# Two pairs of gate/up groups, each by seven products of 512 columns, in place of four single groups by seven products of 256

## The chip, the cores and the metric

The kernel runs on one core of one Trainium2 chip. The metric is the device time of one execution in microseconds. In three runs the kernel before took 278.68, 278.72 and 279.11 us, with a median of 278.72 us. One execution was recorded by the hardware profiler: it took 278.33 us, of which the instructions span 276.6 us, at a mean granted TensorE clock of 0.995. All times of instructions below are of that execution, in us from the start of the span.

The engines are named as in the profile: PE (TensorE; PEld is its weight load), DVE (VectorE), ACT (ScalarE), POOL (GpSimd) and SP (the engine whose queue issues most loads).

## The reference

The program is one transformer block on 256 tokens of width 1024, all in float32:

```python
u = rms_norm(h, mix_norm_g[l])
proj = u @ w_in[l]                      # q, k, v, glu_a, glu_g
attn_out = moba_attention(heads(q), heads(k), heads(v), rel_bias)
conv_out = conformer_conv(glu_a, glu_g, ...)
h = h + concatenate([attn_out, conv_out]) @ w_out[l]
u = rms_norm(h, ffn_norm_g[l])
h = h + (silu(u @ w_gate[l]) * (u @ w_up[l])) @ w_down[l]
return rms_norm(h, final_norm_g)
```

The change lies in the feed-forward part, the last two lines but one: `u @ w_gate` and `u @ w_up` are products of 256 x 1024 by 1024 x 2816, and `w_down` is 2816 x 1024.

## The kernel before

**Precision.** Every float32 operand is cut into a high part, which a cast rounds to the multiply format (ACT, `act.copy`), and a low part, the rest (DVE, `vec.tensor_sub`). A product is three matmuls: high by high, high by low, low by high. Tiles `wh_*` are the high parts of weights; all low parts lie in nine slots of one tile, `wl`. `split(name)` makes both parts of one loaded block, `high(name, i)` only the high part of one half. A loaded block (`raw_*`) is two halves of 128 x 1024 elements, 512 KB each.

**Groups.** The 2816 columns of gate and up are 11 groups `g` of 256 columns. A plain group (`gate_up`) takes 48 matmuls of 512 moving columns, 256 of gate and 256 of up side by side, into two PSUM banks `pf`, one for each 128 tokens. `swiglu` takes Silu on ACT (`fs`) and the product on DVE (`ff`).

**Seven products.** Groups 4, 6, 8 and 10 (`SG`) are computed by a seven-multiplication scheme of Strassen's kind instead: the 256 tokens are two blocks, the depth of 1024 two blocks, the columns two blocks, and instead of eight block products there are seven, of sums of blocks. The sums of token blocks are made once (`sums_of_blocks`, tile `sf`). The sums of weight blocks, seven *forms* for each group, are made on DVE (`ft` tiles hold them) and cut into high and low parts as other weights are (`form`; tiles `wh_m*`). Each of the seven products is 12 matmuls of 256 columns. ACT copies finished products out of PSUM and DVE adds them (`cp` tiles). `first_forms`, `middle_forms` and `last_forms` stand at three places ahead of the products; the parts of a group are made one to two groups ahead.

**Way back to the down projection.** The gated product `ff` must be turned, tokens against columns. `send(g)` transposes blocks on DVE (`fv`), writes them to DRAM from POOL's queue (`fd`) and reads them back in four transfers (`fb`). `land(g)` makes their high part on ACT (`fh`) and low part on DVE (`fl`). `down(g, ...)` is 24 matmuls of 512 columns for a group, added up over all groups in four PSUM banks `pd`. Each product of `down` is three matmuls, by `fh` and `wh_d`, `fh` and `wl`, then `fl` and `wh_d`.

**Order.** The order on each engine is the order of the program text (`tc.keep_in_program_order`): an instruction whose input is late holds up all that stand behind it on its engine. The loop over groups writes, for each `g`: `swiglu(g)` and `send(g)`, the products of group `g+1`, the parts of group `g+2`, `land(g-1)` and `down(g-1)`. Loads are issued by SP in the order of the list `order` as buffers come free: `raw` has room for three blocks. PSUM has four banks beside those of `pd`, taken in turn (`spare`). `h_turn`, `h_rows` and `h_back` turn the residual stream through DRAM for the end (tiles `hb`, `ht`); two of its eight transposes on DVE are made in each of groups 1 to 4.

Of the kernel before, what the change touches and what calls it, by code (L numbers as in the profile page):

```python
# [15 lines left out]
P = 128  # L16
# [26 lines left out]
SG = (4, 6, 8, 10)  # L43
MIX = 48

# [19 lines left out]
def block_kernel(ctx, tc, xT, w_in, w_out, w_gu, w_down, pvec, gfin, relb, hot, out):  # L65
# [37 lines left out]
    for g in range(FG + 2):  # L103
        if g < FG:
            order += [(w_gu, 4096 * g, f"g{g}"), (w_gu, 4096 * g + 2048, f"u{g}")]
        if g > 1:
            order += [(w_down, 2048 * (g - 2), f"d{g - 2}")]
# [161 lines left out]
    def diagonal(rc, name):  # L269
        dg = const.tile([P, S], F32, name=f"dg_{name}", tag="dg")  # L270
# [10 lines left out]
    def sumsq(a, src, k, n):  # L281
        if k == 0:
            act.activation(a, src, AF.Square)
        else:
            sq = const.tile([P, S], F32, name=f"sq_{n}{k}", tag="sq", bufs=3)
            act.activation(sq, src, AF.Square)
            vec.tensor_add(a, a, sq)
# [113 lines left out]
    def bias_parts():  # L401
        pzs.append(const.tile([2 * NB, S], F32R, name="hot_r", tag="sq", bufs=3))
# [281 lines left out]
    def seven_products(g):  # L684
# [5 lines left out]
        kept = [w2.tile([P, 512], F32, name=f"cp{g}{i}", tag="fsq", bufs=2) for i in range(2)]  # L690
# [32 lines left out]

    def swiglu(g):
# [143 lines left out]
    def square_rows(t, i, lo, hi):  # L868
        sq = w2.tile([P, 512], F32, name=f"fsq{t}{i}", tag="fsq", bufs=2)
# [10 lines left out]
    def last_columns(t):  # L880
# [11 lines left out]
        sq = w2.tile([P, 512], F32, name=f"fsq{t}2", tag="fsq", bufs=2)  # L892
# [77 lines left out]
def _layout(x, mix_norm_g, w_in, rel_bias, conv_w, conv_b, conv_ln_g, conv_ln_b, w_out,  # L970
# [13 lines left out]
    gu = _in_turns(np.concatenate(pairs, axis=3)).reshape(P, FG, -1)  # L984
    for n in SG:
# [34 lines left out]
```

## Time and profile before

| what | value |
|---|---|
| median of 3 runs | 278.72 us |
| the profiled execution | 278.33 us |
| its span, first to last instruction | 276.6 us |
| PE / DVE / ACT / POOL busy, share of the span | 97% / 88% / 66% / 19% |
| one plain group on PE | 10.36 us |
| one group by seven products on PE | 9.38 us |
| one group's down projection on PE | 5.18 us |
| the feed-forward products begin / the last one by seven products ends | 109.44 / 253.25 us |

The profile's rows give a start, a length, the engine, the operation and the tiles it writes and reads (`out<-in`), how many instructions are merged, and in brackets how long the engine had been idle and what released it. Instructions on DVE and ACT overlap a little at their ends, so what one costs in a row of them is the step from start to start, not the length. The chain of waits is followed back from the last instruction; a chain that stays on one engine without a break means that this engine set the end.

### The profile page before, as it was taken

The page shows a single profiled execution, that of the slowest core. Times are in us where ns is not written, and L with a number is a line of the kernel's source. Part 1 is how long each engine was busy: PE and PEld are TensorE (multiplying, and loading weights), DVE is VectorE, ACT ScalarE, POOL GpSimd, SP SyncE. Part 2 cuts the span into 40 slices and gives each one's busy share as a digit, 9 for nine tenths or more (in the row PEclk, how much of TensorE's full clock was granted, in tenths as well). Part 3 has the DMA queues.
Part 4 walks back from the last instruction along what each step waited for, and adds up shares of the span by engine and source line. Part 5 has one row for each costly group of instructions (what it writes and reads, how often), then busy time and mean ns, then how long its engine had stood idle before and what let it go on. Part 6 is the DMA issues. An engine that isn't in the chain of part 4 may idle for free.

```text
span 276.6 us, 5114 instructions
## 1 busy us (share of the span) xinstructions
PE 268.0 (97%) x1845; PEld 243.1 (88%) x1845; DVE 243.2 (88%) x432; ACT 183.5 (66%) x317; POOL 52.0 (19%) x89
## 2 busy tenths in 40 slices
PE   8999999999999999999999999999999999999990
PEld 8999996996899998888888998899888998899880
DVE  3998999999977789979999699998969998988684
ACT  4894676996796678779655566657647684766331
POOL 2011000041001000331421403140430413140052
PEclk9999999999999999999999999999999999999998
DMA  7999899999938455894995468969894688961012
GB/s 219 346 378 346 302 242 277 359 251 221 294 120 261 144 196 162 290 368 135 317 382 182 154 213 283 331 169 283 254 393 142 217 292 309 354 236 28 0 47 105
DMA packets 22811, 66.38 MB, mean 240 GB/s; under 512 B 3258, under 2 KB 6274, under 8 KB 22786
## 3 DMA queue, kind: packets, MB, share of 16 engines
q1 hardware_dynamic: 18754, 55.08, 58.6%
q0 software_dynamic: 3600, 10.57, 14.6%
q10 hardware_dynamic: 432, 0.41, 0.4%
q8 instruction: 14, 0.23, 0.3%
q14 instruction: 11, 0.09, 0.1%
HBM read 58.10 MB, written 5.32 MB: 229 GB/s over the span
## 4 chain that ended last, share of the span: by engine, by line
PE 90%; DVE 4%; DMA 1%; issue 1%; ACT 1%; SPq 1%; POOL 0%; POOLq 0%; DVEq 0%; ACTq 0%
PE pf L77 23%; PE pd L77 19%; PE ps L77 15%; PE py L77 8%; PE pqk L77 8%; PE pv L77 4%; PE pa L77 4%; PE pg L77 3%; PE pc L77 3%; DMA raw_a<-in_w_in 1%; PE pt L80 1%; DVE acch L88 1%; PE po L77 1%; DVE hg L88 1%; DVE wl L88 1%
## 5 line engine op out<-in xcount | busy, mean ns | idle before, releaser
L77 PE MATMUL pf<-wl,us 128*128 128x512 f32 x112 | 42.4, 379 | 0.0
L77 PE MATMUL pf<-wh_u,us 128*128 128x512 f32 x112 | 34.7, 380 | 0.0
L77 PE MATMUL pf<-wh_g,us 128*128 128x512 f32 x112 | 34.5, 379 | 0.0
L77 PE MATMUL pd<-wh_d,fh 128*128 128x512 f32 x84 | 32.0, 381 | 0.0
L88 POOL DMA_DIRECT2D fb<-fd x40 | 23.2, 586 | 46.7 <-issue 25.1
L77 PE MATMUL pd<-wl,fh 128*128 128x512 f32 x84 | 31.8, 379 | 0.0
L77 PE MATMUL pd<-wh_d,fl 128*128 128x512 f32 x84 | 31.8, 379 | 0.0
L88 DVE TENSOR_TENSOR wl<-raw_d,wh_d 128x1024 fp32r<-128x1024 f32 x22 | 26.1, 1214 | 2.7 <-ACT wh_d L88 2.3
L88 ACT CAST wh_m<-ft 128x1024 fp32r<-128x1024 f32 x16 | 16.8, 1048 | 15.3 <-DVE ft L88 15.2
L77 PEld LDWEIGHTS pf<-wh_g,us 128*128 128x128 f32 x112 | 21.2, 189 | 3.0
L77 PEld LDWEIGHTS pf<-wh_u,us 128*128 128x128 f32 x112 | 21.2, 189 | 3.0
L77 PEld LDWEIGHTS pf<-wl,us 128*128 128x128 f32 x112 | 21.2, 189 | 3.0
L88 ACT CAST wh_d<-raw_d 128x1024 fp32r<-128x1024 f32 x22 | 22.6, 1048 | 0.9 <-DMA raw_d<-in_w_down 0.6
L77 PE MATMUL ps<-wh_m,sf 128*128 128x256 f32 x128 | 22.7, 275 | 0.0
L77 PE MATMUL pqk<-us,wh_qk 128*128 128x256 f32 x128 | 21.7, 276 | 0.0
L77 PEld LDWEIGHTS ps<-wh_m,sf 128*128 128x128 f32 x128 | 20.1, 192 | 0.0
L77 PEld LDWEIGHTS pqk<-us,wh_qk 128*128 128x128 f32 x128 | 19.5, 192 | 0.5 <-issue 0.4
L88 DVE SCALAR_TENSOR_TENSOR cacc<-upad,pv,cacc 128x256 f32<-128x256 f32 x48 | 19.8, 479 | 0.0
L88 DVE TENSOR_TENSOR wl<-ft,wh_m 128x1024 fp32r<-128x1024 f32 x16 | 19.0, 1212 | 0.0
L77 PE MATMUL ps<-wh_m,us 128*128 128x256 f32 x96 | 18.0, 275 | 0.0
L77 PE MATMUL py<-mh,wh_o 128*128 128x256 f32 x64 | 18.0, 281 | 0.0
L77 PEld LDWEIGHTS pd<-wh_d,fl 128*128 128x128 f32 x84 | 15.9, 189 | 2.2
(184 smaller groups left out, 736.2 us busy)
## 6 DMA issues: line engine op xcount, KB each, us to landing
raw_g<-in_w_gu SPq DMA_DIRECT2D x22, 512.0 KB, 5.0
raw_u<-in_w_gu SPq DMA_DIRECT2D x22, 512.0 KB, 5.1
raw_d<-in_w_down SPq DMA_DIRECT2D x22, 512.0 KB, 5.6
raw_qk<-in_w_in SPq DMA_DIRECT2D x8, 512.0 KB, 7.3
raw_o<-in_w_out SPq DMA_DIRECT2D x8, 512.0 KB, 6.4
raw_a<-in_w_in SPq DMA_DIRECT2D x12, 256.0 KB, 4.2
fd<-fv POOLq DMA_DIRECT2D x10, 256.0 KB, 4.8
fb<-fd POOLq DMA_DIRECT2D x40, 64.0 KB, 4.7
```

Source lines behind the costliest of these rows:

```text
L77: return tc.keep_in_program_order(nc.tensor.matmul(*args, **kw))
L80: return tc.keep_in_program_order(nc.tensor.transpose(o, i, ident))
L88: return lambda *a, **k: tc.keep_in_program_order(f(*a, **k))
```

## The change

Groups 4+5 and 8+9 (the program counts from zero) are now computed in pairs (`PAIRS`), groups 6 and 10 become plain, and `SG` is empty. So there are seven plain groups before and after, and four groups by seven products.

In a pair the column blocks are gate and up of both groups, 512 columns each. Each form is 512 deep by 512 wide, that is two halves of 128 x 1024 elements (`form(g, (i, n), ...)`), and each product is two half products of 6 matmuls of 512 columns (`half_product`). The pair has 14 halves of forms and 8 passes for sums, as two single groups had. Its products fill four PSUM banks (`x`, `y`, `z`, `w`); the copies, sums and gates work on 512 columns at a time.

The forms are split round a plain group's product: form 0 and the first sums stand behind the plain group's parts (`first_of_pair`), form 1 ahead of that group's `swiglu` (`forms_of_sums`), forms 2 and 3 and the other sums behind it (`middle_of_pair`), and forms 4, 5 and 6 inside the products, ahead of the first three (`late`). `down` of two groups follows a pair. `send` of a pair issues both writes ahead of the reads. The residual's transposes move: two in each of groups 1 and 2, four in group 6, with `h_rows` and `h_back` there too. Some small tiles change pools, and `hb`, `ht` and the unsummed blocks share one buffer.

```diff
@@ -40,8 +40,11 @@
 WARM = 9
 SHIFT = 16
 PLACE = 112
-SG = (4, 6, 8, 10)
+PAIRS = (4, 8)
+SG = ()
 MIX = 48
+TURNS = {1: (0, 1), 2: (2, 3), 6: (4, 5, 6, 7)}
+ROWS, BACK = 6, 6
 
 PROGRAM = """
...
@@ -100,11 +103,12 @@
     places.update({f"v{i}": (w_in, 16384 + 2048 * i) for i in range(2)})
     places.update({f"o{i}": (w_out, 2048 * i) for i in range(4)})
     order = [(*places[t[1]], t[1]) for t in steps if t[0] == "ld" and t[1] in places]
-    for g in range(FG + 2):
-        if g < FG:
-            order += [(w_gu, 4096 * g, f"g{g}"), (w_gu, 4096 * g + 2048, f"u{g}")]
-        if g > 1:
-            order += [(w_down, 2048 * (g - 2), f"d{g - 2}")]
+    units = [(g, g + 1) if g in PAIRS else (g,) for g in range(FG) if g - 1 not in PAIRS]
+    for unit in units:
+        names = ("ga", "gb", "gd", "gc") if len(unit) > 1 else ("g", "u")
+        order += [(w_gu, 4096 * unit[0] + 2048 * i, f"{n}{unit[0]}") for i, n in enumerate(names)]
+        order += [(w_down, 2048 * (g - 2), f"d{g - 2}") for g in unit if g > 1]
+    order += [(w_down, 2048 * g, f"d{g}") for g in range(FG - 2, FG)]
     order.reverse()
     raws, parts = {}, {}
     low = wts.tile([P, 9 * HW + 128], F32R, name="wl", bufs=1)
...
@@ -647,10 +655,39 @@
             form(g, 4 + i, raw)()
 
 
+    def first_of_pair(g):
+        a, b, d = (take(n + str(g)) for n in ("ga", "gb", "gd"))
+        for n in range(2):
+            form(g, (0, n), a[n])()
+        t = [[w2.tile([P, HW], F32, name=f"ft{g}{i}{n}", tag="ft", bufs=4) for n in range(2)] for i in range(2)]
+        for n in range(2):
+            vec.tensor_sub(t[0][n], b[n], a[n])
+        for n in range(2):
+            vec.tensor_sub(t[1][n], d[n], b[n])
+        raw4[g] = t, d
+
+    def forms_of_sums(g, i):
+        lows = [form(g, (1 + i, n), raw4[g][0][i][n]) for n in range(2)]
+        for low_part in lows:
+            low_part()
+
+    def middle_of_pair(g):
+        t, d = raw4[g]
+        c = take(f"gc{g}")
+        forms_of_sums(g, 1)
+        for n in range(2):
+            vec.tensor_sub(t[0][n], d[n], t[0][n])
+        for n in range(2):
+            form(g, (3, n), c[n])()
+        for n in range(2):
+            vec.tensor_sub(t[1][n], c[n], t[0][n])
+        raw4[g] = t[0], d, t[1]
+
     sums = []
...
@@ -721,6 +758,79 @@
             send(g)
             split(f"u{g + 1}")
 
+    def half_product(o, g, i, n, uh, ul, start):
+        wh, wl = forms[g, (i, n)]
+        for k in (2 * n, 2 * n + 1):
+            h, l = (in_turns(w[:, k % 2 * 512 : k % 2 * 512 + 512]) for w in (wh, wl))
+            mm(o, uh[:, k], h, start=start and k == 0, stop=False, skip_group_check=True)
+            mm(o, uh[:, k], l, start=False, stop=False, skip_group_check=True)
+            mm(o, ul[:, k], h, start=False, stop=k == 3, skip_group_check=True)
+
+    def pair_products(g):
+        sf = sums[1]
+        u = [[tuple(p[:, 4 * k : 4 * k + 4, t * P : (t + 1) * P] for p in (hh, hl)) for k in range(2)] for t in range(2)]
+        m = [(sf[:, i, 0], sf[:, i, 1]) for i in range(4)]
+        x, y, z, w = (bank(next(spare), f"ps{n}{g}") for n in "xyzw")
+        s1, s5, s7, su = (w2.tile([P, 512], F32, name=f"cp{g}{i}", tag="fsq", bufs=4) for i in range(4))
+        first, second, nxt = f"d{g - 2}", f"d{g - 1}", g + 2
+
+        def late(i, n):
+            form(g, (i, n), raw4[g][i - 4][n])()
+
+        def gate(t, a, b):
+            act.activation(a, a, AF.Silu, scale=rc2[:, t : t + 1])
+            for i in range(2):
+                ff[g + i, t] = a[:, i * S : (i + 1) * S]
+            return lambda: vec.tensor_mul(a, a, b)
+
+        late(4, 0)
+        half_product(x, g, 0, 0, *u[0][0], True)
+        late(4, 1)
+        half_product(x, g, 0, 1, *u[0][0], True)
+        act.copy(s1, x)
+        land(g - 2)
+        late(5, 0)
+        half_product(y, g, 1, 0, *m[0], True)
+        late(5, 1)
+        half_product(y, g, 1, 1, *m[0], True)
+        act.copy(s5, y)
+        late(6, 0)
+        half_product(z, g, 2, 0, *m[2], True)
+        late(6, 1)
+        half_product(z, g, 2, 1, *m[2], True)
+        act.copy(s7, z)
+        split(first, 0)
+        half_product(w, g, 3, 0, *u[0][1], True)
+        split(first, 1)
+        vec.tensor_add(s5, s5, s7)
+        half_product(w, g, 3, 1, *u[0][1], True)
+        vec.tensor_add(s1, w, s1)
+        split(second, 0)
+        half_product(x, g, 4, 0, *m[1], False)
+        high(second, 1)
+        half_product(x, g, 4, 1, *m[1], False)
+        act.copy(su, x)
+        split(second, 1)
+        high(f"g{nxt}", 0)
+        vec.tensor_add(s5, s5, su)
+        half_product(y, g, 5, 0, *m[3], False)
+        high(f"g{nxt}", 1)
+        split(f"g{nxt}", 0)
+        half_product(y, g, 5, 1, *m[3], False)
+        vec.tensor_add(s7, y, su)
+        one = gate(0, s1, s7)
+        one()
+        split(f"g{nxt}", 1)
+        half_product(z, g, 6, 0, *u[1][1], False)
+        land(g - 1)
+        high(f"u{nxt}", 0)
+        half_product(z, g, 6, 1, *u[1][1], False)
+        vec.tensor_add(su, z, su)
+        two = gate(1, su, s5)
+        two()
+        send(g, g + 1)
+        split(f"u{nxt}")
...
@@ -733,12 +843,17 @@
     fd = [dram.tile([4, 2, P, 2 * 32], F32, name=f"fd{n}") for n in range(3)]
     fb = {}
 
-    def send(g):
-        fv = w2.tile([P, 4, 2, 2 * 32], F32, name=f"fv{g}", tag="fv", bufs=2)
-        for t in range(2):
-            vec.transpose(fv[:, :, t], ff[g, t])
+    def send(*groups):
+        for g in groups:
+            fv = w2.tile([P, 4, 2, 2 * 32], F32, name=f"fv{g}", tag="fv", bufs=2)
+            for t in range(2):
+                vec.transpose(fv[:, :, t], ff[g, t])
+            pool.dma_start(fd[g % 3].rearrange("b t p c -> p (b t) c"), fv.rearrange("p b t c -> p (b t) c"))
+        for g in groups:
+            receive(g)
+
+    def receive(g):
         d = fd[g % 3]
-        pool.dma_start(d.rearrange("b t p c -> p (b t) c"), fv.rearrange("p b t c -> p (b t) c"))
         fb[g] = w2.tile([P, 2, 4, 2, 32], F32, name=f"fb{g}", tag="fb", bufs=3)
         for b in range(4):
             pool.dma_start(fb[g][32 * b : 32 * b + 32].rearrange("p t a i s -> p (t a) (i s)"),
...
@@ -804,44 +921,54 @@
 
 
 
-    for g in range(FG):
-        if g not in SG:
+    for unit, after, then in zip(units, units[1:] + [()], units[2:] + [(), ()]):
+        g = unit[-1]
+        ahead = len(then) > 1
+        shared = [n[0] for n in (after, then) if n]
+        shared = [n in SG or n in PAIRS for n in shared] + [False, False]
+        if not (g in SG or len(unit) > 1 or len(after) > 1):
             swiglu(g)
-            if g < FG - 1:
+            if after:
                 send(g)
-        if g + 1 in SG:
+        if len(after) > 1:
+            pair_products(g + 1)
+        elif shared[0]:
             last_forms(g + 1)
             seven_products(g + 1)
         else:
-            if g < FG - 1:
+            if after:
                 gate_up(g + 1)
-            if 0 < g < FG - 1:
+            if g > 0 and (after or g not in SG):
                 split(f"d{g - 1}")
-            if g + 2 in SG:
-                first_forms(g + 2)
-            elif g < FG - 2:
-                split(f"g{g + 2}")
+            if shared[1]:
+                first_forms(then[0])
+            elif then:
+                split(f"g{then[0]}")
             if g > 0:
                 land(g - 1)
-        if 0 < g < FG - 2:
-            for i in range(2):
-                for t in range(2):
-                    for n in range(2):
-                        down(g - 1, i, t, n * 512, n * 512 + 512)
-        if g + 2 in SG:
-            middle_forms(g + 2)
-        elif g < FG - 2 and g + 1 not in SG:
-            split(f"u{g + 2}")
+        for n in range(g - 1, g - 1 + len(after)):
+            if 0 <= n < FG - 3:
+                for i in range(2):
+                    for t in range(2):
+                        for c in range(2):
+                            down(n, i, t, c * 512, c * 512 + 512)
+        if ahead:
+            forms_of_sums(then[0], 0)
+            swiglu(g + 1)
+            send(g + 1)
+        if shared[1]:
+            middle_forms(then[0])
+        elif then and not shared[0]:
+            split(f"u{then[0]}")
         if g == 0:
             sums_u()
             sums_of_blocks()
-        if g == 8:
+        for m in TURNS.get(g, ()):
+            h_turn(m)
+        if g == ROWS:
+            h_rows()
+        if g == BACK:
             h_back()
-        if 1 <= g <= 4:
-            h_turn(2 * g - 2)
-            h_turn(2 * g - 1)
-        if g == 4:
-            h_rows()
     split(f"d{FG - 1}")
 
 
```

How the instructions stand now. First DVE, around the end of a pair's products. In front of the low parts `fl3`, which down(3) reads, there stood before (`u5` and `g6` are blocks of gate/up weights, `d3` of down weights, `ft6*` sums for the forms of group 6):

```order
L88 TENSOR_TENSOR wl_69<-raw_u5_0_2001,wh_u5_0_2109 128x1024
L88 TENSOR_TENSOR wl_69<-raw_u5_1_2002,wh_u5_1_2110 128x1024
L88 STREAM_TRANSPOSE hb_1495<-xs_70 128x8x32 x2
L88 TENSOR_TENSOR wl_69<-raw_d3_0_2050,wh_d3_0_2195 128x1024
L88 TENSOR_TENSOR wl_69<-raw_d3_1_2051,wh_d3_1_2196 128x1024
L88 TENSOR_TENSOR wl_69<-raw_g6_0_2105,wh_m6_0_2209 128x1024
L88 TENSOR_TENSOR ft60_2212<-raw_g6_1_2106,raw_g6_0_2105 128x1024
L88 TENSOR_TENSOR ft61_2213<-raw_u6_1_2192,raw_g6_1_2106 128x1024
L88 TENSOR_TENSOR fl3_2217<-fb3_1951,fh3_2216 128x256 x2
```

In the changed program the last rows up to `fl3` are these (`psw4`, `psy4` are products of the pair that begins with group 4, `cp4*` its copies):

```order
L91 TENSOR_TENSOR wl_69<-raw_d2_0_1887,wh_d2_0_2055 128x1024
L91 TENSOR_TENSOR wl_69<-raw_d2_1_1888,wh_d2_1_2056 128x1024
L91 TENSOR_TENSOR cp41_1985<-cp41_1985,cp42_1986 128x512
L91 TENSOR_TENSOR cp40_1984<-psw4_1983,cp40_1984 128x512
L91 TENSOR_TENSOR wl_69<-raw_d3_0_1958,wh_d3_0_2079 128x1024
L91 TENSOR_TENSOR wl_69<-raw_d3_1_1959,wh_d3_1_2080 128x1024
L91 TENSOR_TENSOR cp41_1985<-cp41_1985,cp43_1987 128x512
L91 TENSOR_TENSOR wl_69<-raw_g6_0_2051,wh_g6_0_2102 128x1024
L91 TENSOR_TENSOR cp42_1986<-psy4_1981,cp43_1987 128x512
L91 TENSOR_TENSOR cp40_1984<-cp40_1984,cp42_1986 128x512
L91 TENSOR_TENSOR wl_69<-raw_g6_1_2052,wh_g6_1_2103 128x1024
L91 TENSOR_TENSOR fl3_2131<-fb3_1953,fh3_2130 128x256 x2
```

Before, the matmuls of group 5 lay between group 4's products and down(3); now down(2) and down(3) follow the pair's products directly, and `fl3` stands behind the parts of two down groups, the pair's sums and both low parts of `g6`.

Second POOL's queue, where the groups are sent through DRAM. Before:

```order
L88 DMA fd0_1491<-fv3_1947 128x8x64
L88 DMA fb3_1951<-fd0_1491 32x8x64 x4
L88 DMA fd1_1492<-fv4_2096 128x8x64
L88 DMA fb4_2100<-fd1_1492 32x8x64 x4
L88 DMA hd_1496<-hb_1495 32x8x256 x4
L88 DMA fd2_1493<-fv5_2271 128x8x64
```

Now:

```order
L91 DMA fd0_1491<-fv3_1949 128x8x64
L91 DMA fb3_1953<-fd0_1491 32x8x64 x4
L91 DMA fd1_1492<-fv4_2152 128x8x64
L91 DMA fd2_1493<-fv5_2156 128x8x64
L91 DMA fb4_2160<-fd1_1492 32x8x64 x4
L91 DMA fb5_2165<-fd2_1493 32x8x64 x4
L91 DMA fd0_1491<-fv6_2339 128x8x64
```

Groups 4 and 5 are sent together: both writes stand ahead of the first read, and `fv4` is made when the pair's products are finished.

Third DVE, from a plain group's gate to the products behind it. Before, for group 5 ahead of the seven products of group 6:

```order
L88 TENSOR_TENSOR ff50_2265<-fs50_2263,pf50_2141 128x256
L88 TENSOR_TENSOR ff51_2269<-fs51_2267,pf51_2142 128x256
L88 STREAM_TRANSPOSE fv5_2271<-ff50_2265 128x4x64
L88 STREAM_TRANSPOSE fv5_2271<-ff51_2269 128x4x64
L88 TENSOR_TENSOR wl_69<-ft60_2212,wh_m6_4_2280 128x1024
L88 TENSOR_TENSOR wl_69<-raw_u6_1_2192,wh_m6_5_2283 128x1024
L88 TENSOR_TENSOR wl_69<-ft61_2213,wh_m6_6_2286 128x1024
L88 TENSOR_TENSOR fl4_2307<-fb4_2100,fh4_2306 128x256 x2
L88 TENSOR_TENSOR wl_69<-raw_d4_0_2201,wh_d4_0_2329 128x1024
```

Now, for group 7 ahead of the pair 8+9:

```order
L91 STREAM_TRANSPOSE fv7_2478<-ff70_2472 128x4x64
L91 STREAM_TRANSPOSE fv7_2478<-ff71_2476 128x4x64
L91 TENSOR_TENSOR wl_69<-ft810_2428,wh_m8_(2, 0)_2491 128x1024
L91 TENSOR_TENSOR wl_69<-ft811_2429,wh_m8_(2, 1)_2493 128x1024
L91 TENSOR_TENSOR ft800_2426<-raw_gd8_0_2408,ft800_2426 128x1024
L91 TENSOR_TENSOR ft801_2427<-raw_gd8_1_2409,ft801_2427 128x1024
L91 TENSOR_TENSOR wl_69<-raw_gc8_0_2412,wh_m8_(3, 0)_2499 128x1024
L91 TENSOR_TENSOR wl_69<-raw_gc8_1_2413,wh_m8_(3, 1)_2502 128x1024
L91 TENSOR_TENSOR ft810_2428<-raw_gc8_0_2412,ft800_2426 128x1024
L91 TENSOR_TENSOR ft811_2429<-raw_gc8_1_2413,ft801_2427 128x1024
L91 STREAM_TRANSPOSE hb_1799<-xs_70 128x8x32 x4
L91 TENSOR_TENSOR wl_69<-ft800_2426,wh_m8_(4, 0)_2526 128x1024
```

Behind the plain group's `fv` there were three low parts of forms; now there are forms 2 and 3 with the remaining sums (eight passes over 1024 columns), four transposes of the residual and then form 4.

More of the change, by code (lines that the diff above doesn't have):

```diff
@@ L269, in diagonal @@
     def diagonal(rc, name):
-        dg = const.tile([P, S], F32, name=f"dg_{name}", tag="dg")
+        dg = w1.tile([P, S], F32, name=f"dg_{name}", tag="dg")
         for t in range(2):
@@ L284, in sumsq @@
         else:
-            sq = const.tile([P, S], F32, name=f"sq_{n}{k}", tag="sq", bufs=3)
+            sq = w1.tile([P, S], F32, name=f"sq_{n}{k}", tag="sq", bufs=3)
             act.activation(sq, src, AF.Square)
@@ L401, in bias_parts @@
     def bias_parts():
-        pzs.append(const.tile([2 * NB, S], F32R, name="hot_r", tag="sq", bufs=3))
+        pzs.append(w1.tile([2 * NB, S], F32R, name="hot_r", tag="sq", bufs=3))
         vec.tensor_copy(pzs[0], hot_s)
@@ L626, in first_forms @@
     def first_forms(g):
+        if g in PAIRS:
+            return first_of_pair(g)
         a, b = take(f"g{g}")
@@ L629, in first_forms @@
         form(g, 0, a)()
-        t = [w2.tile([P, HW], F32, name=f"ft{g}{i}", tag="hg", bufs=2) for i in range(2)]
+        t = [w2.tile([P, HW], F32, name=f"ft{g}{i}", tag="ft", bufs=4) for i in range(2)]
         vec.tensor_sub(t[0], b, a)
@@ L635, in middle_forms @@
     def middle_forms(g):
+        if g in PAIRS:
+            return middle_of_pair(g)
         t, c, d = raw4[g]
@@ L647, in last_forms @@
             form(g, 4 + i, raw)()
+    def first_of_pair(g):
[23 more added lines that the diff above has]
+        raw4[g] = t[0], d, t[1]
     sums = []
     def sums_u():
-        u = [w2.tile([P, 4, S], F32, name=f"fu{i}", tag="hg", bufs=2) for i in range(2)]
+        whole = w2.tile([P, KD, S], F32, name="fu", tag="hb", bufs=1)
+        u = [whole[:, 4 * i : 4 * i + 4] for i in range(2)]
         sf = w2.tile([P, PLACE + 4096], F32R, name="sf")
@@ L689, in seven_products @@
         x, z, y, w = (o[:, i : i + S] for o in (one, two) for i in (0, S))
-        kept = [w2.tile([P, 512], F32, name=f"cp{g}{i}", tag="fsq", bufs=2) for i in range(2)]
+        kept = [w2.tile([P, 512], F32, name=f"cp{g}{i}", tag="fsq", bufs=4) for i in range(2)]
         s1, s5, s7, su = (o[:, i : i + S] for o in kept for i in (0, S))
@@ L777, in down @@
         mm(o, fl, wh, start=False, stop=stop, skip_group_check=True)
-    ht = w2.tile([P, 2, D], F32, name="ht")
-    hb = w2.tile([P, KD, KD, 32], F32, name="hb")
+    taken = {}
     hd = dram.tile([S, D], F32, name="hd")
     def h_turn(m):
-        tc.keep_in_program_order(vec.transpose(hb[:, :, m], xs[:, m].rearrange("p (b j) -> p b j", j=32)))
+        if m == 0:
+            taken["t"] = w2.tile([P, KD, KD, 32], F32, name="hb", tag="hb", bufs=1)
+        tc.keep_in_program_order(vec.transpose(taken["t"][:, :, m], xs[:, m].rearrange("p (b j) -> p b j", j=32)))
     def h_rows():
@@ L789, in h_rows @@
             tc.keep_in_program_order(pool.dma_start(bass.AP(tensor=hd.tensor, offset=hd.offset + a * S, ap=[[D, 32], [32 * D, KD], [1, S]]),
-                           hb[32 * a : 32 * a + 32].rearrange("p b m j -> p b (m j)")))
+                           taken["t"][32 * a : 32 * a + 32].rearrange("p b m j -> p b (m j)")))
     def h_back():
+        ht = taken["h"] = w2.tile([P, 2, D], F32, name="ht", tag="hb", bufs=1)
         for t in range(2):
@@ L858, in block_kernel @@
     a, b = FG - 2, FG - 1
+    ht = taken["h"]
     ends = []
@@ L868, in square_rows @@
     def square_rows(t, i, lo, hi):
-        sq = w2.tile([P, 512], F32, name=f"fsq{t}{i}", tag="fsq", bufs=2)
+        sq = w2.tile([P, 512], F32, name=f"fsq{t}{i}", tag="fsq", bufs=4)
         act.activation(sq[:, : hi - lo], ht[:, t, lo:hi], AF.Square, accum_out=ends[t]["ss"][:, i : i + 1])
@@ L891, in last_columns @@
         vec.scalar_tensor_tensor(ms[:, 0:1], ss[:, 1:2], 1.0 / D, ms[:, 0:1], op0=ALU.mult, op1=ALU.add)
-        sq = w2.tile([P, 512], F32, name=f"fsq{t}2", tag="fsq", bufs=2)
+        sq = w2.tile([P, 512], F32, name=f"fsq{t}2", tag="fsq", bufs=4)
         vec.tensor_tensor_reduce(out=sq[:, 0:S], in0=ht[:, t, 768:1024], in1=ht[:, t, 768:1024], scale=1.0 / D, scalar=ms[:, 0:1],
@@ L984, in _layout @@
     gu = _in_turns(np.concatenate(pairs, axis=3)).reshape(P, FG, -1)
+    for n in PAIRS:
+        gate, up = (_in_turns(w[:, n : n + 2].transpose(0, 2, 1, 3).reshape(P, KD, 2 * S)) for w in pairs)
+        gu[:, n : n + 2] = np.stack([gate[:, :4], up[:, :4], up[:, 4:], gate[:, 4:]], axis=1).reshape(P, 2, -1)
     for n in SG:
```

2 lines of the change are left out of this document (1 added, 1 removed).

## The prediction, made before the changed kernel ran

> **What bounds the kernel now.** I read the page first (busy shares and the chain's shares), then the chain of waits in order of time, then the busy times by stretch, and last the timelines of VectorE (DVE), ScalarE (ACT) and the queues.
>
> ```profile
> PE 268.0 (97%) x1845; PEld 243.1 (88%) x1845; DVE 243.2 (88%) x432; ACT 183.5 (66%) x317; POOL 52.0 (19%) x89
> PE 90%; DVE 4%; DMA 1%; issue 1%; ACT 1%; SPq 1%; POOL 0%; POOLq 0%; DVEq 0%; ACTq 0%
> ```
>
> The chain of waits (start, length, what) is one unbroken run of matmuls in the second half:
>
> ```profile
> 138.04 10.36 PE pf L77 x48
> 148.40 5.18 PE pd L77 x24
> 153.58 9.38 PE ps L77 x84
> 162.96 5.18 PE pd L77 x24
> 168.14 10.36 PE pf L77 x48
> ...
> 253.25 2.59 PE pd L77 x12
> ```
>
> `pf` is a plain gate/up group, `ps` seven products, `pd` a down projection. Each row starts where the one before ends, so PE never waits, and whatever takes matmul time away or makes PE wait counts one for one. VectorE is the next candidate. The stretch table (length, sum, then PE, PEld, DVE, ACT, POOL) for one seven group plus one plain group:
>
> ```profile
> 153.60:183.70 30.10, 30.10 (x182) 27.52 (x182) 27.18 (x40) 19.18 (x27) 6.93 (x12) 1.00 0.73 233
> ```
>
> VectorE is busy 27.18 of 30.10 us, and over the whole change its work stays nearly the same. What matters is how that work lies against the products, which only an account in its queue's order shows.
>
> **What the matmuls save.** A 512-column matmul costs 10.36/48 = 0.2158 us, a 256-column one in `ps` 9.38/84 = 0.1117. Four seven groups were 4 x 9.38 = 37.52; the two pairs are 2 x 84 x 0.2158 = 36.26. **Gain 1.26 us** if PE never waits. One pair takes 18.13, a half product 1.295. Seven groups are plain before and after, the down projections are untouched: the joint width is the only gain in matmul time.
>
> [...]
>
> **VectorE up to the first pair.** Nothing that VectorE issues before 138.91 is changed. Its rows of before (start, length; the step to the next row is what one costs):
>
> ```profile
> 138.91 1.22 DVE L88 TENSOR_TENSOR wl<-raw_g,wh_m 128x1024 fp32r<-128x1024 f32 x1
> 140.04 1.22 DVE L88 TENSOR_TENSOR ft<-raw_g,raw_g 128x1024 f32<-128x1024 f32 x1
> 141.81 1.23 DVE L88 TENSOR_TENSOR ft<-raw_u,raw_g 128x1024 f32<-128x1024 f32 x1 [0.55 <-DMA raw_u<-in_w_gu]
> 142.95 0.76 DVE L88 TENSOR_TENSOR fl<-fb,fh 128x256 fp32r<-128x256 f32 x2
> 143.62 2.35 DVE L88 TENSOR_TENSOR wl<-ft,wh_m 128x1024 fp32r<-128x1024 f32 x2
> 145.90 1.22 DVE L88 TENSOR_TENSOR ft<-raw_u,ft 128x1024 f32<-128x1024 f32 x1
> ...
> 149.30 0.77 DVE L88 STREAM_TRANSPOSE hb<-xs 128x256 f32<-128x256 f32 x2
> 149.99 0.71 DVE L88 TENSOR_TENSOR ff<-fs,pf 128x256 f32<-128x256 f32 x2
> 150.63 0.75 DVE L88 STREAM_TRANSPOSE fv<-ff 128x256 f32<-128x256 f32 x2
> ```
>
> and, for 512 columns, the two rows
>
> ```profile
> 123.47 2.49 DVE L88 TENSOR_TENSOR sf<-fu,sf 128x512 fp32r<-128x512 f32 x4
> 125.88 0.74 DVE L88 TENSOR_TENSOR ff<-fs,pf 128x256 f32<-128x256 f32 x2
> ```
>
> So a pass over 1024 columns takes 1.135 (138.91 to 140.04 for one, 143.62 to 145.90 for two), a couple over 256 columns 0.64 to 0.69, a pass over 512 columns 2.41/4 = 0.60. These prices carry over: the changed passes have the same shapes, except that the sums and gates double to 512.
>
> Before the pair, the loads come in. `gd4` takes the place in SP's queue that `d2` had, behind the same freed buffer:
>
> ```profile
> 137.88 1.46 SPq L88 DMA_DIRECT2D raw_d<-in_w_down  x2
> DMA to landing us min/median/max: 5.9/5.9/6.0
> DMA to landing us min/median/max: 3.5/5.8/8.2
> ```
>
> (the second line is of these two transfers; the third of the `raw_u` pair between 175 and 190 us, the widest spread seen). So `gd4` lands at 143.8 and 145.0. VectorE: two low parts and two `gb - ga` from 138.91 to 143.45, the two `gd - gb` wait 0.4 in all and end at 146.1, `fl1` 146.8, low parts of form 1 149.1. Then `ff3`, whose input is ready at 148.97:
>
> ```profile
> 148.50 0.47 ACT L88 ACTIVATE fs<-pf,rc_h 128x256 f32<-128x256 f32 x1 [0.17 <-PE pf L77]
> 139.97 0.71 ACT L88 CAST fh<-fb 128x256 fp32r<-128x256 f32 x2 [2.03 <-DMA fb<-fd]
> L88 ACT CAST sf<-fu 128x512 fp32r<-128x512 f32 x4 | 2.3, 617 | 1.6 <-DVE fu L88 1.6
> ```
>
> **First stall, in down(3).** From `ff3` to the first half of `fl3` VectorE issues, in order: 4 short passes (1.31), 8 long (forms 2 and 3 and their sums), `hb` 0.69, 2 long (form 4), `fl2` 0.67, 4 long (forms 5, 6), 2 long (`d2`), two 512 sums, 2 long (`d3`), one 512 sum, 1 long, two 512, 1 long (`g6`), `fl3` 0.42. That is 20 x 1.135 + 5 x 0.60 + 3.09 = 28.8 us, so `fl3` is there at 149.1 + 28.8 = 177.9. PE: 153.58 + 18.13 + 5.18 (down 2) = 176.89, and the third matmul of down(3), the first that reads `fl3`, at 177.32. **PE waits 0.6.** The forms themselves come in time: form 5's first low part is ready at 164.4 for 166.5, the tightest. In before the same `fl3` had a whole plain group between. Bounds: without the 0.4 us of DMA wait 0.2; with landings of 8.2 us, 2.3 more: 2.8. I take 0.6, since the transfer keeps its place and its company.
>
> **Second stall, in down(4).** Behind `fl3` (both halves 178.16) come the last sum (178.85 with its latency), ACT's Silu over 512 (0.62, as the cast above: 179.47), the gate's product 180.07 and two transposes: 180.8. Only now POOL can send group 4, and `fd4`, `fd5` stand ahead of the loads back. What one trip takes:
>
> ```profile
> 127.60 0.90 POOL L88 DMA_DIRECT2D fd<-fv  x1 [3.21 <-DVE fv L88]
> 131.62 2.31 POOL L88 DMA_DIRECT2D fb<-fd  x4 [3.12 <-DMA fd<-fv]
> 137.04 0.89 POOL L88 DMA_DIRECT2D fd<-fv  x1 [3.12 <-DVE fv L88]
> 143.28 2.31 POOL L88 DMA_DIRECT2D fb<-fd  x4 [5.34 <-DMA fd<-fv]
> DMA to landing us min/median/max: 2.2/4.7/6.9
> ```
>
> The first trip ended with ACT's `fh` at 139.97 (quoted above): 12.37 us. So `fh4` starts at 193.2 and is ready at 193.6; PE ends down(3) at 182.07 + 0.6 and the plain group 6 10.36 later, at 193.03. **PE waits 0.55.** Bounds: 4.0 to 6.2 (fd to fb) + 1.74 (four issues) + 2.2 to 6.9 gives trips of 7.9 to 14.8, a wait of 0 to 3.0. I take the one trip that was seen to its end. VectorE stands idle behind this wait: `fl4` stands ahead of `u7`, `ff6`, `d5` and all forms of pair 8, so nothing of the idle time is used.
>
> **Third stall, in down(7).** Counting from 193.6: `fl4` 0.67; `u7` waits for its casts behind `fh4` on ACT (0.68) and takes 2.27; `ff6`, `fv6` 1.31; `d5` 2.27; form 0 2.27; four sums 4.54 with 0.3 of DMA wait; `fl5` 0.67; form 1 2.27: `ff7` starts at 210.8. Its input is there at 193.6 + 5.18 + 10.36 + 0.57 = 209.7 (0.57 as from 148.40 to 148.97). From there the list of the first stall again, with four `hb` transposes instead of two: 28.8 + 0.69 = 29.5, so `fl7` at 240.3. PE: 193.6 + 5.18 + 10.36 + 5.18 + 18.13 + 5.18 + 0.43 = 238.05. **PE waits 2.2.** Bounds: VectorE on time at `ff7` (start 209.4) 0.8; a landing of 8.2 us, 4.5. I take the account's 2.2.
>
> Down(8) follows a shorter trip with few loads left: 0, at most 0.6 by the 12.37 trip. The end (from 253.25 on) is the same program in the same order; the `hd`/`ht` transfers move later on POOL's queue, between `fb7` and `fd8`, and `fd8` comes over 10 us after them. The pair holds all four spare PSUM banks; the next plain group reuses those of `x` and `y`, read out by ACT's copy and by the 512 sum at about 176, 6 us before it starts: no wait.
>
> **Sum.** 278.33 (profiled execution: span 276.6 and 1.73 around it) - 1.26 + 0.6 + 0.55 + 2.2 = 280.4. The median of the runs, 278.72, stands 0.4 above the profiled one: **280.8 us**, 0.7% slower.
>
> **Rivals.**
> - *VectorE keeps ahead (faster).* If it reaches `fl3` and `fl7` before PE, only the gain stays: 278.72 - 1.26 = 277.5. It decides in pair 8, where even with `ff7` on time 0.8 is missing: the 20 long passes would have to cost under 1.095. For it: 2.9 us of idle VectorE in the stretch table; against it: that idle time lay inside the old seven products, where the new order has none. 0.13.
> - *Stalls at their lower bounds (same).* Loads land early: 0.2 + 0 + 0.8 - 1.26 = -0.3, 278.4. 0.20.
> - *The trip through DRAM decides.* Two sends and eight loads back beside SP's loads: 3.0 in down(4) instead of 0.55: 283.3. For it, DMA share 0.73 in the stretch table; 0.12.
> - *512 columns bring nothing*, since the products switch weights and halves more often than `pf`: 282.1. Against it: `pd` switches weights every two matmuls too, at 5.18/24 = 0.2158. 0.05.
>
> [...] Since the trip's own bound is 3.0, this gets 0.02 of its 0.12.
>
> **How the numbers follow.** The forecast holds 0.50. About 0.2% (0.56 us) is what a measurement here tells from no change. Faster 0.13; same 0.20; slower 0.50 + 0.12 + 0.05 = 0.67. The forecast's own range is 279.4 to 282.5; with the same-case below and the trip above, 278.0 to 283.6 leaves out the first rival and the joined upper ends.
>
> **What would show it.** Right: 84 matmuls of a pair in 18.1 us plus waits; PE idle ahead of `pd<-...fl` at the end of each pair's second down, released by VectorE's `fl`, and a wait of ACT's `fh` for `fb` ahead of down(4) with VectorE idle beside it. Wrong: PE without gaps (then the rows' steps or the order mislead me), a wait inside the products (a form late), or at a plain group's start (a bank or a load of `g6`).

## The result, and the profile after

The changed kernel takes **282.14 us** (median of four runs, 281.39 to 282.45), the kernel before 278.83 beside it (278.68 to 279.11): ratio 1.0114, 95% interval 1.0096 to 1.0132. It is 1.1% slower. Of all runs below one, of 286.59 us, was over 1.5% slower than the fastest of its kernel, and its ratio leaves it out. The forecast was 280.8, range 278.0 to 283.6, slower with a chance of 0.67. The profiled execution of the changed kernel took 282.10 with a span of 280.0.

The page's busy shares and the chain's shares:

```profile
PE 267.9 (96%) x1677; PEld 237.3 (85%) x1677; DVE 241.4 (86%) x418; ACT 181.1 (65%) x305; POOL 52.3 (19%) x89
PE 60%; DVE 14%; DMA 12%; issue 5%; ACT 3%; SPq 2%; POOL 2%; POOLq 0%; DVEq 0%; ACTq 0%
```

There are 168 matmuls fewer, PE is busy as long as before, and PE's share of the chain has fallen from 90% to 60%: in places PE now waits. The chain of waits (start, length, what) of the changed kernel:

```profile
138.90 10.36 PE pf L80 x48
149.26 5.18 PE pd L80 x24
154.44 2.59 PE psx L80 x12
...
187.19 6.99 DMA fb<-fd
...
241.22 5.02 PE pd L80 x22
246.23 10.36 PE pf L80 x48
256.59 2.59 PE pd L80 x12
```

Twelve joint matmuls take 2.59, as the plain ones do (2.59/12 = 0.2158), and the whole pair takes 18.13, as this stretch shows (length, sum, then PE, PEld, DVE, ACT, POOL):

```profile
154.44:172.57 18.13, 18.13 (x85) 15.88 (x85) 18.13 (x21) 15.48 (x20) 2.32 (x4) 1.00 0.52 169
```

PE is never interrupted inside the products, and VectorE is busy for every microsecond of them. PE's timeline has three gaps in the whole feed-forward part; the bracket is the idle time and what ended it:

```profile
177.80 0.38 PE L80 MATMUL pd<-wl,fh 128*128 128x512 f32 x1
178.70 0.48 PE L80 MATMUL pd<-wh_d,fl 128*128 128x512 f32 x1 [0.52 <-DVE fl L91]
179.02 0.38 PE L80 MATMUL pd<-wh_d,fh 128*128 128x512 f32 x1
...
194.69 0.48 PE L80 MATMUL pd<-wh_d,fh 128*128 128x512 f32 x1 [0.62 <-ACT fh L91]
...
239.07 0.38 PE L80 MATMUL pd<-wl,fh 128*128 128x512 f32 x1
241.22 0.48 PE L80 MATMUL pd<-wh_d,fl 128*128 128x512 f32 x1 [1.76 <-DVE fl L91]
241.54 0.38 PE L80 MATMUL pd<-wh_d,fh 128*128 128x512 f32 x1
```

They are in down(3), down(4) and down(7), the three places of the forecast. What one costs is read from the starts: 177.80 to 178.70 is 0.90 where 0.22 is usual, so 0.68; and 178.70 to 179.02 is 0.32, so another 0.10. The same reading gives 0.87 in down(4), where the third matmul takes 0.04 more (0.91 in all), and 2.03 in down(7).

VectorE's timeline at these places:

```profile
149.68 0.74 DVE L91 TENSOR_TENSOR ff<-fs,pf 128x256 f32<-128x256 f32 x2
...
177.09 1.22 DVE L91 TENSOR_TENSOR wl<-raw_g,wh_g 128x1024 fp32r<-128x1024 f32 x1
178.23 0.75 DVE L91 TENSOR_TENSOR fl<-fb,fh 128x256 fp32r<-128x256 f32 x2
...
180.37 0.69 DVE L91 TENSOR_TENSOR cp<-cp,cp 128x512 f32<-128x512 f32 x1 [0.79 <-ACT cp L91]
...
211.54 0.75 DVE L91 TENSOR_TENSOR ff<-fs,pf 128x256 f32<-128x256 f32 x2
...
240.75 0.75 DVE L91 TENSOR_TENSOR fl<-fb,fh 128x256 fp32r<-128x256 f32 x2
```

From `ff3` (149.68) to `fl3` (178.23) are 28.55 us, from `ff7` to `fl7` 29.21; between them VectorE's rows stand back to back, but for one step: from the sum that reads `psy` to the product behind it are 0.79 (175.69 to 176.48, and the same in the second pair), where the other 512-column steps are 0.60. These are the two lists of the forecast. Its 28.8 and 29.5 reach to the end of the first half of `fl`, 0.42 further; from start to start it has 28.4 and 29.1.

The wait in down(4) is that for the trip through DRAM, from POOL's write to ScalarE's cast, 12.20 us:

```profile
182.04 1.78 POOL L91 DMA_DIRECT2D fd<-fv  x2 [24.84 <-DVE fv L91]
194.24 0.71 ACT L91 CAST fh<-fb 128x256 fp32r<-128x256 f32 x2 [9.16 <-DMA fb<-fd]
```

From PE's first down projection behind the mixing to the tail, the chain's rows run from 132.86 to 253.25 before, 120.39 us, and from 133.72 to 256.59 after, 122.87. The first rows of the two, before and after:

```profile
132.86 5.18 PE pd L77 x24
133.72 5.18 PE pd L80 x24
```

The difference of 2.48 is -1.26 + 3.73, the gain and the three waits. The medians differ by 3.3; the other 0.8 is, by these two profiles, outside this part: the profile after is 0.86 later already at the first down projection, and its time is 2.1 above its span where the one before has 1.73.

### The profile page after: what moved, and what is told of

Its sections match the earlier page's. It is cut to its first block, busy times and chain, and to the rows that moved or that the text cites. A ratio compares the mean times of both kernels' runs of the same rounds, so it can differ in the third digit from the quotient of the medians.

```text
span 280.0 us, 4740 instructions
## 1 busy us (share of the span) xinstructions
PE 267.9 (96%) x1677; PEld 237.3 (85%) x1677; DVE 241.4 (86%) x418; ACT 181.1 (65%) x305; POOL 52.3 (19%) x89
## 4 chain that ended last, share of the span: by engine, by line
PE 60%; DVE 14%; DMA 12%; issue 5%; ACT 3%; SPq 2%; POOL 2%; POOLq 0%; DVEq 0%; ACTq 0%
PE pf L80 16%; PE pd L80 10%; PE py L80 8%; PE pqk L80 8%; DVE wl L91 6%; PE pv L80 4%; DMA raw_a<-in_w_in 3%; PE pc L80 3%; DMA ht<-hd 3%; DVE ft L91 3%; DMA fb<-fd 2%; DMA hd<-hb 2%; PE psy L80 2%; PE psx L80 2%; SPq L91 2%
## 5 line engine op out<-in xcount | busy, mean ns | idle before, releaser
L91 POOL DMA_DIRECT2D fd<-fv x10 | 9.1, 909 | 66.3 <-DVE fv L91 63.7
L91 ACT CAST fh<-fb 128x256 fp32r<-128x256 f32 x20 | 7.1, 405 | 18.5 <-DMA fb<-fd 18.5
L80 PEld LDWEIGHTS pd<-wh_d,fh 128*128 128x128 f32 x84 | 15.9, 189 | 3.1 <-ACT fh L91 1.0
L80 PE MATMUL pqk<-us,wl 128*128 128x256 f32 x64 | 17.7, 277 | 0.0
L80 PEld LDWEIGHTS pd<-wl,fh 128*128 128x128 f32 x84 | 15.9, 189 | 2.1
```

The source lines that it names most:

```text
L80: return tc.keep_in_program_order(nc.tensor.matmul(*args, **kw))
L91: return lambda *a, **k: tc.keep_in_program_order(f(*a, **k))
```

## The experiments

The theory at this point: PE waits in down(3) and down(7) because `fl` stands too far back in VectorE's queue, and in down(4) because the transposes, and with them the send, come too late for a trip of 12 us. The rivals: loads or the trip itself set these times whatever the order, or the joint products cost it. Each experiment is shown as an edit of the changed kernel, where nothing else is said.

### The landing earlier

```
         split(second, 1)
+        land(g - 1)
         high(f"g{nxt}", 0)
         ...
         half_product(z, g, 6, 0, *u[1][1], False)
-        land(g - 1)
         high(f"u{nxt}", 0)
```

> Only change against the changed kernel: inside each pair's products, the cast and the low part of the activations for the second down projection (fh, fl of groups 3 and 7) are issued three positions earlier, ahead of the low parts of the next plain group. Theory (VectorE's queue order ahead of fl is what PE waits for): fl is ready 3 to 4 us earlier, so the 0.79 us of waiting in down(3) and the 2.03 us in down(7) go. The sums, gates and transposes behind it end when they did, so the send starts when it did and fh of group 4 comes when it did: the wait in down(4) grows from 0.91 to 1.7 us by what was saved ahead of it. Net 2.0 us less: 280.1 (between 279.8 and 280.5). Rival (the loads from HBM or the casts on ScalarE set the time of fl, not VectorE's queue): fl moves by less than 1 us and the time stays within 0.5 us of 282.1. Second rival (the waits are the price of the wide products themselves, the order is of no account): 282.1.

Measured: 280.24 us (12 runs, 279.11 to 281.12), ratio to before 1.0038, interval 1.0023 to 1.0054. PE has one gap left in the feed-forward part:

```profile
194.58 0.48 PE L80 MATMUL pd<-wh_d,fh 128*128 128x512 f32 x1 [0.78 <-ACT fh L91]
```

VectorE's timeline now has the low parts at 174.41 and 236.36:

```profile
174.41 0.76 DVE L91 TENSOR_TENSOR fl<-fb,fh 128x256 fp32r<-128x256 f32 x2
236.36 0.76 DVE L91 TENSOR_TENSOR fl<-fb,fh 128x256 fp32r<-128x256 f32 x2
```

They come 3.8 and 4.4 us earlier, though no load, cast or product is cheaper, and both waits are gone. The edit moves the cast `fh3` on ScalarE as well, but in the changed kernel that was done at 173.1 (it starts at 172.44 and takes 0.70), 5 us ahead of `fl3`. So it was the place in VectorE's queue. The remaining gap costs 1.04 (0.94 and 0.10) in this profile, not 1.7: this execution's trip took 11.62 us (`fd` at 182.50, the cast at 194.12), 0.58 less than that of the changed kernel. The median is 0.14 above the 280.1 expected, though with a smaller last wait than was reckoned; the openings differ by more than that between executions (below), so the wait's size is not confirmed by it, only that two waits went and one stayed.

### The low parts of the next group behind the send

```
         high(f"g{nxt}", 1)
-        split(f"g{nxt}", 0)
         ...
         one()
-        split(f"g{nxt}", 1)
         ...
         send(g, g + 1)
+        split(f"g{nxt}")
         split(f"u{nxt}")
```

> Only change against the changed kernel: the two low parts of the next plain group's gate block (2.27 us of VectorE) are issued behind the gates' transposes and the send, not between the sums; everything else stays. Theory (VectorE's list up to fl and up to the transposes is too long by these two passes): fl of groups 3 and 7, the transposes and the send come 2.27 us earlier. The wait of 0.79 in down(3), of 0.91 in down(4) and of 2.03 in down(7) all go, no wait at the start of the plain groups 6 and 10 takes their place (the low parts are ready 0.4 to 0.6 us ahead of their products): 3.7 us less, 278.4. If the later low parts come late after all: up to 0.5 us per pair, 279.4. Rival (the trip through DRAM is stretched by SP's loads, so an earlier send brings no earlier landing): the wait in down(4) stays at 0.9 to 1.7, 279.3 to 280.1. Second rival (the waits do not hang on the order): 282.1.

Measured: 278.64 us (12 runs), ratio 0.9988, interval 0.9969 to 1.0008: no difference from before that can be measured, and 3.5 under the changed kernel. The three gaps are gone, the plain groups start on time, and PE's timeline shows one small gap that was not there, in down(8):

```profile
252.31 0.38 PE L80 MATMUL pf<-wh_u,us 128*128 128x512 f32 x1
252.89 0.48 PE L80 MATMUL pd<-wh_d,fh 128*128 128x512 f32 x1 [0.20 <-ACT fh L91]
253.21 0.38 PE L80 MATMUL pd<-wl,fh 128*128 128x512 f32 x1
```

It costs 0.46: PE now comes there 4 us earlier, the cast `fh8` only 1.7 (252.43, for 254.16 in the changed kernel). Moving two passes over 1024 columns, without making anything cheaper, gives back the whole loss. For group 4 an earlier send brings an earlier landing: `fd` at 179.72, the cast at 191.22, a trip of 11.50. For group 8 the rival is half right: the write comes 4.0 us earlier (240.59 for 244.56), but the trip takes 11.84 in place of 9.60. What stretches it was not tried.

### The landing later

The opposite of the first edit, to see the same cause with a larger size.

```
-        land(g - 1)
         high(f"u{nxt}", 0)
         ...
         send(g, g + 1)
+        land(g - 1)
         split(f"u{nxt}")
```

> Only change against the changed kernel, the opposite of the earlier landing: inside each pair's products the cast and low part for the second down projection (fh, fl of groups 3 and 7) are issued behind the gates' transposes and the send. By VectorE's rows of the changed kernel (last sum 0.60, 0.79 of waiting, gate 0.61, four transposes 1.37) fl comes 3.45 us later: the pause in down(3) grows from 0.79 to 4.2 us, the one in down(4) goes, since PE is later than the trip, and the one in down(7) grows from 2.03 to over 4. By the queue order alone, matmuls at full speed: 287.0. By the queue order and a clock that is halved after a pause of some 3 us (as the variant with the sends one by one has shown after 3.07 us: six matmuls 0.43 us apart, 1.4 us lost), twice 1.4 us and what the second pair's list loses by the later start: 290.3. If VectorE's order is not what sets fl: 282 to 283.

Measured: 291.34 us (four runs, 290.37 to 291.62), ratio 1.044, interval 1.0421 to 1.0459. PE's timeline in down(3):

```profile
177.42 0.38 PE L80 MATMUL pd<-wh_d,fl 128*128 128x512 f32 x1
180.02 0.48 PE L80 MATMUL pd<-wh_d,fh 128*128 128x512 f32 x1 [2.23 <-ACT fh L91]
180.34 0.38 PE L80 MATMUL pd<-wl,fh 128*128 128x512 f32 x1
182.09 0.79 PE L80 MATMUL pd<-wh_d,fl 128*128 128x512 f32 x1 [1.37 <-DVE fl L91]
182.68 0.63 PE L80 MATMUL pd<-wh_d,fh 128*128 128x512 f32 x1
183.11 0.63 PE L80 MATMUL pd<-wl,fh 128*128 128x512 f32 x1
```

The wait came in two pieces, since the cast `fh` now stands behind a Silu on ScalarE as well; together 3.91, 4.01 with the first matmul's 0.10, for 4.2 expected. After it the matmuls are 0.43 apart instead of 0.22, until 188.19: those 14 steps take 6.10 us, so 3.08 are lost. In down(7) it is 2.93 and 1.54 of waiting and 1.79 by slow matmuls. The stretch table of PE (length, PE busy with its matmuls counted, granted clock, DMA share, GB/s) has a granted clock of 0.50 there:

```profile
178.00:180.00 2.00, 0.00 (x0) 1.00 0.78 248
180.00:182.00 2.00, 0.70 (x2) 0.83 0.50 184
182.00:184.00 2.00, 1.91 (x5) 0.50 0.45 174
```

The queue order at full clock gave 287.0, with two slow stretches 290.3; the runs decide for the second. What was wrong is their size: 1.4 each was expected, from the one profile seen by then; it was 3.08 and 1.79.

### The two groups sent one after the other

```
             pool.dma_start(fd[g % 3]...)
-        for g in groups:
             receive(g)
```

> Only change against the changed kernel: a pair's two groups are sent one after the other, fd of group 4 and its four loads back, then fd of group 5 and its loads, where the changed kernel writes both before the first load back. Theory (the trip is 4 us of landing and 7 us of loads back, and the second write stood only in the shade of the first one's landing): fh of group 4 comes 0 to 0.5 us earlier, the wait in down(4) is 0.4 to 0.9 us, total 281.6 to 282.1. Rival (the second write and the eight loads back crowd the first ones out): fh of group 4 comes over 1 us earlier, the wait in down(4) goes, total 281.2 or less. The waits in down(3) and down(7) stay at about 0.8 and 2.0 by both, except that down(7)'s grows by as much as PE gains without VectorE.

Measured: 283.82 us (six runs, 281.98 to 286.59), ratio 1.0151, interval 1.0126 to 1.0177. Both expectations missed the total. On the disputed point the theory holds: the cast of group 4 starts at 193.56 after a write at 181.88, a trip of 11.68 for 12.20, so not the 1 us shorter of the rival, and the wait in down(4) falls from 0.91 to 0.4. The second write and its loads do not crowd the first ones out. Whether the 0.52 is owed to the edit at all is open: in the four other variants, which send both groups together, the trip took 11.28 to 11.79.

What cost more lies behind it. Group 5's loads back are now issued at 195.90, where they were issued from about 187.8 on, and fall together with SP's load of `raw_gd`, which takes 6.6 us and more to land, for 5.4 and 5.5 in the changed kernel. That the loads beside it are the cause is not shown: with the low parts behind the send it took up to 6.4 without them. This load is in the chain of waits (start, length):

```profile
200.09 6.64 DMA raw_gd<-in_w_gu
```

VectorE's timeline has the wait for it:

```profile
206.75 2.44 DVE L91 TENSOR_TENSOR ft<-raw_gd,raw_gb 128x1024 f32<-128x1024 f32 x2 [1.01 <-DMA raw_gd<-in_w_gu]
```

In the changed kernel the same pair of passes started at 206.33 without a wait. So `fl7` is 0.51 later, PE is there 0.63 earlier, and the gap in down(7) grows from 2.03 to 3.17. Then the clock, in PE's timeline:

```profile
241.73 0.80 PE L80 MATMUL pd<-wh_d,fl 128*128 128x512 f32 x1 [2.91 <-DVE fl L91]
242.32 0.63 PE L80 MATMUL pd<-wh_d,fh 128*128 128x512 f32 x1
242.74 0.63 PE L80 MATMUL pd<-wl,fh 128*128 128x512 f32 x1
```

and in this kernel's stretch table (same columns as above) the granted clock falls:

```profile
240.00:242.00 2.00, 0.27 (x1) 0.79 1.02 401
242.00:244.00 2.00, 2.00 (x5) 0.50 1.01 387
```

In the changed kernel, with its gap of 1.93, the same stretch has full clock:

```profile
240.00:242.00 2.00, 0.78 (x4) 1.00 1.03 418
```

The slow matmuls lose 1.40 beyond the usual 0.10. Down(3)'s gap is 1.00 here, 0.22 more. Sum: +0.22 - 0.51 + 1.14 + 1.40 = 2.25; the feed-forward parts of the two profiles differ by 2.3.

### The small tiles alone

Kernel before, with the pools of three small tiles changed as in the change:

```
-        dg = const.tile([P, S], F32, name=f"dg_{name}", tag="dg")
+        dg = w1.tile([P, S], F32, name=f"dg_{name}", tag="dg")
```

and the same for `sq` and `hot_r`.

> Kernel before with one part of the change alone: the small tiles dg, sq and hot_r come from the pool w1 and not from const; the feed-forward part is that of before. It is about the 0.86 us by which the changed kernel's profile is later already before the feed-forward part begins (PE's down(1) at 133.72 instead of 132.86). Theory A (the moved tiles get other neighbours and later freed places, so the opening is longer): 279.5, and PE's first down projection after the mixing at 133.6 to 133.8. Theory B (the opening differs between executions, or for a reason outside these lines): 278.8, and 132.8 to 133.0.

Measured: 278.98 us against 279.00 of before, ratio 0.9999, interval 0.9987 to 1.0012. The moved tiles cost nothing in the median. The profiled execution took 279.88, and its chain of waits shows where the time is:

```profile
134.42 5.18 PE pd L77 x24
```

This first down projection comes 1.56 us after the one in the profile of before, in a program that takes the same time in the median, and what follows it is as long as before. Neither expectation had so late an opening. So the opening differs between executions by more than the 0.86 that was to be explained (the 29 runs of before beside it spread by 1.5 us, 278.47 to 279.98), and the profile of before happened to show an early one.

### A version without waits

The variant with the low parts behind the send, shown as an edit of that variant, with two moves more: the subtraction of the landing between the last sum and the gate's product, where VectorE waits for ScalarE anyway (`land` is told which half to issue; the cast stays where it was), and three transposes of the residual in each of the units 1 and 2.

```
-TURNS = {1: (0, 1), 2: (2, 3), 6: (4, 5, 6, 7)}
+TURNS = {1: (0, 1, 2), 2: (3, 4, 5), 6: (6, 7)}
...
-        land(g - 1)
+        land(g - 1, "high")
         ...
         two = gate(1, su, s5)
+        land(g - 1, "low")
         two()
```

> The variant with the low parts behind the send, and two further moves. One: the low part of the activations for the second down projection (fl of groups 3 and 7, 0.67 us on VectorE) is issued between the last sum and the gate's product, where VectorE waits 0.8 to 1.25 us for ScalarE's Silu anyway, so the transposes and the send come 0.67 us earlier. Two: of the eight transposes of x into hb, three and three stand in the units 1 and 2 and only two in unit 6, so VectorE's list in the second pair is 0.69 us shorter. Theory: what is left of waiting, 0.46 us in down(8) for fh of group 8, goes, since the send of group 8 is up to 1.36 us earlier; fl of groups 3 and 7 stays ahead of PE by 0.1 to 0.8 us. PE then has no wait from the first down projection to the tail, and the feed-forward part is 1.26 us shorter than before: 278.2, 0.2 to 0.4% under the kernel before. Rival (the last send's trip is stretched by the loads beside it, so it lands no earlier): the 0.46 stays, 278.6. Second rival (the shorter list is taken by fl, now late in down(3) or down(7)): up to 0.6 more, 279.2.

Measured: **277.93 us** (8 runs, 277.63 to 278.46), ratio 0.9964, interval 0.995 to 0.9977: faster than before, and 4.2 under the changed kernel with the same matmuls. The chain's shares:

```profile
PE 90%; DVE 3%; DMA 2%; issue 1%; ACT 1%; SPq 1%; POOL 0%; POOLq 0%; DVEq 0%; ACTq 0%
```

The chain's rows, from the first down projection and at the end:

```profile
133.40 5.18 PE pd L80 x24
...
231.82 10.36 PE pd L80 x48
242.18 10.36 PE pf L80 x48
252.54 2.59 PE pd L80 x12
```

PE has no gap from the first down projection to the tail: 252.54 - 133.40 = 119.14, 1.25 less than 120.39 before. That is the forecast gain of 1.26, alone. The two moves were made together; which of them took away the 0.46 in down(8) is not separated.

## Why the prediction was right

The mechanism and its three places were right, and so was down(7) as by far the largest; of the two small waits the forecast had the larger one in down(3), and it came in down(4). The sizes, point by point:

- **Gain.** 1.26 forecast from the rows; a pair takes 18.13, and the version without waits shows the gain by itself (1.25). The rival that 512 columns bring nothing falls with the same rows; its total, 282.1, is the measured one, so the total alone would have spoken for the wrong cause.
- **First stall, down(3).** 0.6 forecast, 0.79 measured. The gap itself is 0.68; 0.10 more go to the matmul behind it, a term that the sum did not have. That the gap came so near is in part luck, as errors cancelled. The list was 28.55 for 28.4. `ff3` began 0.42 behind the start of down(1) in the chain (149.26 to 149.68) and not 0.70 (148.40 to 149.1), since the 0.4 us of waiting for `gd4` did not come. And PE was placed by the chain's starts, which in an unbroken run lie 0.17 behind the rows' (132.86 for the matmul whose row starts at 132.69).
- **Second stall, down(4).** 0.55 forecast, 0.91 measured. The trip was 12.20 for 12.37, but the write came 3.8 us behind the start of `fl3` (178.23 to 182.04) for 3.3 on paper (177.5 to 180.8), the largest part of it between the gate's product and the write; 0.14 more went to the matmuls behind the gap.
- **Third stall, down(7).** 2.2 forecast, 2.03 measured. The list was 29.21 for 29.1, and `ff7` began 16.85 behind PE's restart in down(4) (194.69 to 211.54) for 17.2 on paper.
- **Down(8), the tail, the banks.** Nothing forecast, nothing seen, in the changed kernel. The small tiles, which the prediction did not speak of, cost nothing.

So the waits sum up to 3.73 where 3.35 stood, and 0.3 of the difference are the three restarts. The other 1.0 between 280.8 and 282.14 are not in the feed-forward part. 0.1 is that the median of before, beside the changed kernel, was 278.83 and not 278.72. Some 0.4 lie outside the span: time minus span is 1.7 to 1.8 for the kernel before, 2.1 to 2.2 for the changed one, 2.0 for three variants of it, but 1.7 to 1.9 for the two others. Its cause is open; nothing here was tried on it. The rest, some 0.5, is not placed: the tails of the two profiles are equally long (23.4 us), so it lies in the opening, or in what differs between executions. The eight executions profiled here reach the first down projection between 132.9 and 134.4, and the one of before, from which the sum started, is the earliest of them; whether the changed kernel's opening is later in the median as well, four runs do not tell.

Of the rivals, *VectorE keeps ahead* named the right condition: the version without waits fulfils it by order alone, and its feed-forward part comes out 1.25 shorter as that rival had it. *The trip decides* was wrong in size: 0.9, not 3.0. Of its 0.12, 0.02 stood for a wait so long that the clock falls as well. No run shows that term: in the changed kernel the longest pause is 1.93 and the granted clock behind it stays 1.00, and in two variants the granted clock fell to 0.50, beside pauses of 2.4 to 3.1 us. *Stalls at their lower bounds* fails with the three sizes above.

## What to carry to other kernels

When a change makes the matmuls cheaper but lets a second engine run without a break beside them, go through that engine's queue up to the first instruction that PE reads next, and count: here 28.55 us against 28.4 on paper. Work that is needed late (the next group's parts) belongs behind work that starts a long trip or that PE reads first; two passes of 1.14 us in each pair, in the wrong place, cost 3.5 us, since the first pair paid twice, in the wait for the low part and in the trip through DRAM, and the second once. Pauses of PE of 0.36 to 1.93 us cost their own length and 0.10 us each here, in down(4) 0.14; where the granted clock fell to 0.50, the three stretches lost 1.5 to 3.1 us more.

## What the runs showed of the hardware

**The granted clock was 0.50 in three places of two variants.** The rows at their ends that are not shown above (same columns; the first of the sends one after the other, the others of the landing later):

```profile
244.00:246.00 2.00, 2.00 (x9) 0.85 0.23 92
188.00:190.00 2.00, 2.00 (x11) 0.96 0.75 250
246.00:248.00 2.00, 0.70 (x2) 1.00 1.02 410
248.00:250.00 2.00, 0.68 (x2) 0.90 0.26 102
252.00:254.00 2.00, 2.00 (x9) 0.75 0.96 317
```

If the clock in these rows, and in those with 0.79 and 0.83 above, is taken as either 1.00 or 0.50, it was 0.50 from 241.2 to 244.6 with the sends one after the other, and from 181.3 to 188.2 and from 249.6 to 253.0 with the landing later: 3.4, 6.8 and 3.4 us, an estimate from the rows. The matmuls of 512 columns stood 0.43 us apart there, 0.22 at 1.00.

By the starts of its matmuls, PE paused for 3.07 us at the first place, for 2.38 and 1.53 at the second, for 2.93 and 1.54 at the third, with two matmuls between the two pauses of the last two places. Behind the 2.93 alone the clock was still 1.00 (the row from 246.00), and behind the 1.93 of the changed kernel it stayed 1.00 (the row from 240.00 to 242.00 of that kernel). Whether the length of a pause, the work around it or something else sets this is not shown by these runs.

**The first matmul behind a gap took 0.10 us more** than its neighbours (0.32 to the next start, not 0.22), at 178.70, 194.69 and 241.22 in the changed kernel, at 252.89 with the low parts behind the send and at 180.02 with the landing later, all at full clock.

**The chain of waits can name a transfer that held nothing up.** In the changed kernel it leads from PE's gap at 241.22 back through the transfers `ht<-hd` and `hd<-hb`, although VectorE's rows up to `fl7` stand back to back; the earlier landing, which leaves these transfers alone, took the gap away.
